# One decoder layer on one core: the mixer and branch stage with all five engines in source order instead of two

## The chip, the core and the metric

The kernel is one program on one core of a Trainium2 chip. A core has five engines, each with its own queue of instructions: TensorE (PE in the profile, PEld for its weight loads), VectorE (DVE), ScalarE (ACT), GpSimd (POOL) and SyncE (SP), which here only issues DMAs. An engine takes its queue from the front; an instruction that has to wait for a semaphore holds everything behind it on that engine. The metric is device time in microseconds (us) of one execution; three runs of the kernel before gave 1828.75, 1835.99 and 1836.97, a median of 1835.99.

## The reference

One layer of a decoder trunk is applied to a prompt of 256 tokens and to 8 single tokens ("samples") that continue stored states; the width is 2048, everything is float32. In outline:

```
h = rmsnorm(x) * (1 + sc1) + sh1                  # sc, sh, gt come from silu(c) @ w_ada
z = h @ w_in                                      # one wide projection for three mixers and their gates
A: u, v = gelu(z_uv);  v = layernorm(v);  y_a = u * (causal 128x128 mix of v per group + b)
B: HGRN2 gated linear recurrence, 8 heads of 128  (chunked, decay = exp of cumulative log gates)
C: GLA gated linear recurrence, 4 heads, value width 256
merged = sum over n of sigmoid(z_gate[n]) * (branch[n] @ w_branch[n])
x = x + gt1 * rmsnorm(merged @ w_out)
x = x + gt2 * rmsnorm(square(relu(h2 @ w_mlp_up)) @ w_mlp_down),  h2 as h, with sc2 and sh2
```

Outputs are the new rows of prompt and samples, the final states of both recurrences for prompt and samples, and the normalised v rows of the samples.

## The kernel before

**The large products.** The 264 tokens (256 + 8) are the moving side of every large product, weights are the stationary side. A float32 weight is split in two float32r parts, hi and lo, and a product is three matmuls: hi by hi (L659), hi by lo (L660), lo by hi (L661). The unit of work is the *granule* (function `granule`, L649): 4 row blocks of 128 by 256 columns of a weight, 512 KB, 24 matmuls. All weights of the kernel form one list (`plan`), and `Stream` walks it: SP loads an item of the list into a `raw` buffer (L616), then `split_half` makes the two halves of the item: ACT copies raw to `whi` (L109), DVE subtracts to get `wlo` (L106, both in `split`). There are four `raw` buffers and six half buffers each of `whi` and `wlo`, that is three items. `Stream.ahead` is called before and after the matmuls of each granule. After granule p it writes the split of item p+3 and the load of item p+6 into the source. The halves of item p+3 take the buffers of the halves of item p, so that the first ACT copy can start when PE is in the middle of granule p and the second when it is at its end.

**The work beside them.** The three mixers are Python generators: `mixer_a` (L881), and `mixer_r` (L1121) for two HGRN2 groups of four heads and for GLA. Their small matmuls, transposes and elementwise steps are put between granules. `linear` (L716) calls `background()` after every granule, which is one *tick*: the counter `now` goes up by one, the queue `bg` (mixers) and the queue `bs` (sample states, `samples_r`) are pumped by their current rates, and `slot()` places collected small matmuls (the level matmuls L679, the samples' matmuls L686) and the modulation matmuls of w_ada (L376), whose weights `Rounds.load` fetches (L339, on SP). A bare `yield` in a generator costs one unit of the rate; `yield READY` waits for the next tick; `yield lambda` waits for a condition. In this way the order of the source already has a distance of ticks between a step and its user: the matrices of a level are used two ticks later or more, the sample state of a step three ticks after its load was issued (`FETCHED`), a value row two.

**Places that the prediction uses.** In `mixer_a`: after `to_tokens` of v, a one-column matmul (L896) ends in a copy (L897); then for each of two token halves two `bn_stats` (L902), `bn_aggr` (L904), eleven one-column steps of a reciprocal root (L213 to L219), the normalisation (L908) and two products with rows (L100, L103 by `mul` and `add`); then the same layer norm for the samples, which starts with three copies (L919, L920) and three folds, whose result PE sums over partitions (L244). In `mixer_r`: the copies of the masked level results into `att` (L1183), the blocks of 32 and 64 (L1192, L1195, then PE at L1208), the scaling of the head outputs (a reciprocal root, then L1285) before their transposes (L1294). In `samples_r`: GpSimd fetches a state `st` (L1077) and a value row `vbc` (L1083), ACT scales the state (L1103), DVE adds the outer product (L1105), GpSimd stores it (L1106). Each branch ends with a gate: `branch` (L1334) has tanh on ACT (L1340) and the gated product on DVE (L1347, L1349). `parts_b` and `parts_c` (L1371 and L1378) finish branches B and C: for C two samples' transposes (L1307) with copies (L1308), then for each of two blocks four products (L1385) and one split of the whole block into hi and lo (an ACT copy and a DVE subtraction of 1056 columns). PE then runs four granules of a gate projection before it needs that block.

**What sets the order.** The source is traced once, and a scheduler orders each engine's queue: it takes instructions in source order as its own forecast of times says that they are ready. Inside `tc.manual_schedule(engines=...)` the engines named keep the order of the source. The kernel uses it in stages, and each stage names other engines. The stage at hand starts at L969, where the generators of the mixers are started, and ends at L1404, behind the last branch. Inside it run GLA's projections (`gla_group`), the three branches and both gate projections: 210 granules. PE and GpSimd keep the order of the source there; DVE, ACT and SP have the scheduler's.

Of the kernel before, what the change touches and what calls it, by code (L numbers as in the profile page):

```python
# [57 lines left out]
def hybrid_step_kernel(  # L58
# [67 lines left out]
    order = tc.manual_schedule(engines={mybir.EngineType.PE, mybir.EngineType.SP, mybir.EngineType.Pool})  # L126
# [659 lines left out]
    every = [mybir.EngineType.PE, mybir.EngineType.SP, mybir.EngineType.Pool, mybir.EngineType.DVE, mybir.EngineType.Activation]  # L786
    order = tc.manual_schedule(engines=set(every))
# [19 lines left out]
    order = tc.manual_schedule(engines=set(every[0:3]))  # L807
# [73 lines left out]
    def mixer_a():  # L881
# [71 lines left out]
        for gp in range(4):  # L953
# [12 lines left out]
            )  # L966
            V.scalar_tensor_tensor(u[:, :, 0:NP], yv[:, :, 0:NP], 0.5, u[:, :, 0:NP], ALU.mult, ALU.mult)
            yield
    order = tc.manual_schedule(engines={mybir.EngineType.PE, mybir.EngineType.Pool})  # L969
    order.__enter__()  # L970
    gen_a = mixer_a()
    bg.g.append(gen_a)
# [499 lines left out]
    order = tc.manual_schedule(engines={mybir.EngineType.PE})  # L1472
# [25 lines left out]
    order = tc.manual_schedule(engines={mybir.EngineType.PE, mybir.EngineType.DVE, mybir.EngineType.Activation})  # L1498
# [161 lines left out]
    order = tc.manual_schedule(engines={mybir.EngineType.PE})  # L1660
# [100 lines left out]
```

## Time and profile before

| | before |
|---|---|
| median of three runs | 1835.99 us |
| profiled execution, its own time | 1832.18 us |
| its span | 1830.4 us |
| PE busy in the span | 1788.7 us (98%) |
| DVE busy | 1181.8 us (65%) |
| ACT busy | 1000.3 us (55%) |
| POOL busy | 131.3 us (7%) |
| the stage at hand, first to last large matmul | 293.3 to 1000.4 us |

PE times are pipelined: a matmul is drawn 277 ns long, and in the steady part of the trace one starts every 0.112 us, so that a granule takes 2.7 us. An engine's idle time in brackets, as in [0.73 <-PE mm L660], is what it waited ahead of that instruction, and for whom. PEclk in a window is the clock granted to PE as a share of full speed.

### The profile page before, as it was taken

To read this page: it belongs to the slowest core of one execution; us is meant where nothing else is said; L and a number is where in the kernel's file an instruction comes from. 1 tells how busy PE (TensorE), PEld (TensorE's weight loads), DVE (VectorE), ACT (ScalarE), POOL (GpSimd) and SP (SyncE) were. 2 spreads that over 40 slices of the span, in tenths; PEclk is the share of its full clock that TensorE was granted. 3 is DMA by queue.
4 is the path that set the end of the run, shared out by engine and by line. 5 is a ranking of instruction groups with operands and counts; after the bars stand their busy time and mean duration, and the time that the engine had idled before them with its cause. 6 is when DMAs were issued, how large, how long until landed. Compare 5 with 4: busy or idle time off the path is not lost.

```text
span 1830.4 us, 42186 instructions
## 1 busy us (share of the span) xinstructions
PE 1788.7 (98%) x17012; PEld 1696.5 (93%) x17012; DVE 1181.8 (65%) x2092; ACT 1000.3 (55%) x1818; POOL 131.3 (7%) x210
## 2 busy tenths in 40 slices
PE   6999999999999999999999999999999999999998
PEld 4889999989988999989999989999999999999997
DVE  4566677787576696566555667555666666666666
ACT  5544364666755765654445666555554545454544
POOL 4221000111111101210000000000000000000000
PEclk9999999999999999999999999999999999999999
DMA  9999697788787788897987964777666666666663
GB/s 326 354 343 304 195 304 231 215 266 276 239 287 233 229 270 278 274 323 250 308 254 265 327 180 146 246 256 227 191 197 194 197 194 196 195 195 196 196 196 106
DMA packets 330179, 442.05 MB, mean 242 GB/s; under 512 B 14946, under 2 KB 276944, under 8 KB 329984
## 3 DMA queue, kind: packets, MB, share of 16 engines
q1 hardware_dynamic: 311728, 380.26, 65.0%
q0 software_dynamic: 17184, 57.85, 9.1%
q8 instruction: 133, 2.18, 0.5%
q10 hardware_dynamic: 1072, 1.25, 0.2%
q14 instruction: 62, 0.51, 0.1%
HBM read 427.60 MB, written 11.70 MB: 240 GB/s over the span
## 4 chain that ended last, share of the span: by engine, by line
PE 88%; DMA 2%; DVE 2%; issue 1%; ACT 1%; POOL 0%; DVEq 0%; ACTq 0%; POOLq 0%
PE mm L659 27%; PE mm L661 26%; PE mm L660 26%; PE ada L376 3%; DMA vbc<-vs_d 1%; PE ada L308 1%; DVE wlo L106 1%; PE sm L851 1%; PE sm L1208 1%; PE sm L679 1%; PE sm L686 1%; DMA raw<-in_w_in_dram 0%; DVE b L106 0%; PE sm L1578 0%; ACT whi L109 0%
## 5 line engine op out<-in xcount | busy, mean ns | idle before, releaser
L659 PE MATMUL mm<-b,whi 128*128 128x264 f32 x4624 | 1292.4, 279 | 12.3 <-issue 5.1
L661 PE MATMUL mm<-b,wlo 128*128 128x264 f32 x4624 | 1279.7, 277 | 5.1 <-DVE wlo L106 4.5
L660 PE MATMUL mm<-b,whi 128*128 128x264 f32 x4624 | 1278.8, 277 | 0.8 <-DVE b L106 0.7
L106 DVE TENSOR_TENSOR wlo<-raw,whi 128x512 fp32r<-128x512 f32 x1136 | 774.4, 689 | 489.1 <-ACT whi L109 475.0
L109 ACT CAST whi<-raw 128x512 fp32r<-128x512 f32 x1136 | 691.8, 616 | 644.5 <-DVE wlo L106 331.7
L659 PEld LDWEIGHTS mm<-b,whi 128*128 128x128 f32 x4624 | 875.8, 189 | 53.0 <-issue 28.0
L661 PEld LDWEIGHTS mm<-b,wlo 128*128 128x128 f32 x4624 | 876.2, 189 | 7.3 <-DVE wlo L106 7.2
L660 PEld LDWEIGHTS mm<-b,whi 128*128 128x128 f32 x4624 | 876.2, 189 | 4.4 <-issue 3.0
L103 DVE TENSOR_TENSOR b<-b,mm 128x528 f32<-128x528 f32 (+1 forms) x137 | 95.7, 699 | 24.5 <-PE mm L661 13.0
L1105 DVE SCALAR_TENSOR_TENSOR st<-vbc,b,st 128x128 f32<-128x128 f32 (+1 forms) x96 | 34.2, 390 | 55.2 <-DMA vbc<-vs_d 50.4
L1103 ACT ACTIVATE st<-st,fs 128x128 f32<-128x128 f32 (+1 forms) x96 | 37.1, 430 | 50.5 <-DMA st<-in_state_hgrn_dram 26.9
L488 POOL DMA_DIRECT2D b<-in_w_ada_dram x64 | 46.2, 724 | 126.0 <-PE ada L308 94.4
L376 PE MATMUL ada<-araw,cT 128*32 128x512 f32 x296 | 39.8, 601 | 0.0
L308 PE MATMUL ada<-b,cT 128*32 128x256 f32 (+1 forms) x640 | 35.1, 356 | 2.8 <-DMA b<-in_w_ada_dram 2.6
L100 DVE TENSOR_TENSOR b<-b,b 128x512 f32<-128x512 f32 (+1 forms) x47 | 33.9, 741 | 1.3 <-ACT b L1221 1.0
L1106 POOL DMA_DIRECT2D out_dram<-st x32 | 23.6, 736 | 130.5 <-DVE st L1105 130.5
L308 PEld LDWEIGHTS ada<-b,cT 128*32 128x32 f32 x640 | 17.8, 113 | 14.9 <-DMA b<-in_w_ada_dram 6.2
L376 PE MATMUL ada<-b,cT 128*32 128x512 f32 x216 | 26.2, 594 | 0.0
L106 DVE TENSOR_TENSOR b<-gt,b 128x528 fp32r<-128x528 f32 x32 | 22.7, 710 | 3.2
L106 DVE TENSOR_TENSOR b<-b 128x1024 f32<-128x1024 f32 (+1 forms) x24 | 24.3, 1017 | 0.0
L1632 ACT ACTIVATE b<-vt 128x528 fp32r<-128x528 f32 x32 | 23.0, 719 | 1.0
L106 DVE TENSOR_TENSOR b<-b,b 128x1056 fp32r<-128x1056 f32 (+3 forms) x21 | 20.8, 991 | 4.0 <-ACT b L109 3.8
(344 smaller groups left out, 854.0 us busy)
## 6 DMA issues: line engine op xcount, KB each, us to landing
raw<-in_w_in_dram SPq DMA_DIRECT2D x231, 512.0 KB, 4.8
raw<-in_w_mlp_up_dram SPq DMA_DIRECT2D x128, 512.0 KB, 3.9
raw<-in_w_mlp_down_dram SPq DMA_DIRECT2D x128, 512.0 KB, 3.7
araw<-in_w_ada_dram SPq DMA_DIRECT2D x74, 512.0 KB, 5.7
b<-in_w_ada_dram SPq DMA_DIRECT2D x54, 512.0 KB, 6.6
b<-in_w_ada_dram POOLq DMA_DIRECT2D x48, 512.0 KB, 8.9
raw<-in_w_branch_dram SPq DMA_DIRECT2D x48, 512.0 KB, 4.5
raw<-in_w_out_dram SPq DMA_DIRECT2D x32, 512.0 KB, 5.3
```

The source lines that it names most:

```text
L100: V.tensor_tensor(o, a, b, op=ALU.mult)
L103: V.tensor_tensor(o, a, b, op=ALU.add)
L106: V.tensor_tensor(o, a, b, op=ALU.subtract)
L109: S.copy(hi, src)
L308: T.matmul(acc[32 * j:32 * j + 32, 0:n], cT[:, k, :], w[:, n * j:n * j + n], start=k == 0, stop=k == KT - 1)
L376: T.matmul(self.acc[32 * j:32 * j + 32, :], cT[:, k, :], ws[j // 2][:, j % 2 * 512:j % 2 * 512 + 512], start=k == 0, stop=k == KT - 1)
L488: queue.dma_start(w[:, i], w1[k * P:(k + 1) * P, :, self.k0 * P:(self.k0 + self.n) * P])
L659: T.matmul(o, a, xh(k + j), start=first and j == 0, stop=False)
L660: T.matmul(o, a, xl(k + j), start=False, stop=False)
L661: T.matmul(o, b, xh(k + j), start=False, stop=last and j == n - 1)
L1103: S.activation(st[:, i, :], st[:, i, :], AF.Copy, scale=fs[:, h0 + i, b:b + 1])
L1105: V.scalar_tensor_tensor(st[:, i, :], v[:, i, :], k[:, h0 + i, NP + b:NP + b + 1], st[:, i, :], ALU.mult, ALU.add)
```

## The change

From L969 to the end of the branches the queues of all five engines keep the order of the source. `every` is the list [PE, SP, Pool, DVE, Activation] that an earlier stage already defined. No instruction is added or removed.

```
-    order = tc.manual_schedule(engines={mybir.EngineType.PE, mybir.EngineType.Pool})
+    order = tc.manual_schedule(engines=set(every))
     order.__enter__()
     gen_a = mixer_a()
     bg.g.append(gen_a)
```

More of the change, by code (lines that the diff above doesn't have):

```diff
@@ L968, in mixer_a @@
             yield
-    order = tc.manual_schedule(engines={mybir.EngineType.PE, mybir.EngineType.Pool})
+    order = tc.manual_schedule(engines=set(every))
     order.__enter__()
```

## The prediction

> **What bounds the kernel now.** The page comes first, then the windows of the stage at hand (293.3 to 1000.4 us) and of a steady later stage.
>
> ```profile
> span 1830.4 us, 42186 instructions
> ...
> L106 DVE TENSOR_TENSOR wlo<-raw,whi 128x512 fp32r<-128x512 f32 x1136 | 774.4, 689 | 489.1 <-ACT whi L109 475.0
> L109 ACT CAST whi<-raw 128x512 fp32r<-128x512 f32 x1136 | 691.8, 616 | 644.5 <-DVE wlo L106 331.7
> ```
>
> ```profile
> 293.30:1000.40 707.10, 696.52 (x7156) 648.81 (x7156) 480.58 (x895) 419.93 (x812) 73.05 (x111) 1.00 0.81 263
> 1300.00:1700.00 400.00, 400.00 (x3558) 400.00 (x3558) 250.08 (x370) 201.84 (x330) 0.00 (x0) 1.00 0.65 196
> ```
>
> PE bounds. In the stage it works 696.5 of 707.1 us, so at most 10.6 us of idle can be won there, while nothing limits what can be lost. The steady window gives the pitch: 400 us over 3558 matmuls is 0.112 us, and a granule of 24 takes 2.7 us. A split costs ACT 2 x 0.62 and DVE 2 x 0.69 us per granule; DVE is busy 480.6 us (68%). Next, PE's waits from 360 to 1060 us, and the waits of DVE and ACT for sample states:
>
> ```profile
> PE mm L659 <- issue: 5.1, 2, 2.9
> PE mm L661 <- DVE wlo L106: 4.3, 5, 2.3
> PE mm L659 <- ACT whi L109: 0.3, 1, 0.3
> ```
>
> ```profile
> DVE st L1105 <- DMA vbc<-vs_d: 50.4, 19, 7.4
> ACT st L1103 <- DMA st<-in_state_hgrn_dram: 26.9, 7, 7.2
> ACT st L1103 <- DMA st<-in_state_gla_dram: 16.9, 9, 3.5
> ```
>
> The scheduler put L1103 and L1105 ahead of where the source has them, before their DMAs land: 94.2 us of waiting at the head of DVE's and ACT's queues, with splits behind. One such place, around 675 us, and below it PE's two other gaps over 2 us:
>
> ```profile
> 673.03 0.69 DVE L106 TENSOR_TENSOR wlo<-raw,whi 128x512 fp32r<-128x512 f32 x1
> 678.16 0.88 DVE L1105 SCALAR_TENSOR_TENSOR st<-vbc,b,st 128x256 f32<-128x256 f32 x2 [4.44 <-DMA vbc<-vs_d]
> 675.67 0.91 ACT L1103 ACTIVATE st<-st,fs 128x256 f32<-128x256 f32 x2 [3.14 <-DMA st<-in_state_gla_dram]
> 677.49 1.12 ACT L109 CAST whi<-raw 128x512 fp32r<-128x512 f32 x2
> 678.16 0.38 PE L659 MATMUL mm<-b,whi 128*128 128x264 f32 x1 [2.19 <-issue]
> 565.89 0.27 PE L659 MATMUL mm<-b,whi 128*128 128x264 f32 x1 [2.86 <-issue]
> 807.34 0.38 PE L661 MATMUL mm<-b,wlo 128*128 128x264 f32 x1 [2.26 <-DVE wlo L106]
> ```
>
> PE's gap ahead of 678.16 is called "issue", but it ends when the first cast of 677.49 does: it belongs to the state wait. The "issue" gap ahead of 565.89 comes with no such wait; I leave it where it is.
>
> **The change part by part.** *Nothing is added or removed*, so the sums are waits alone. PE and POOL keep their order.
>
> *Gain: the state waits go.* In source order L1103 and L1105 stand three and two ticks behind the issue of their DMAs and behind the splits of their tick. PE's share of the waits is 4.3 + 0.3 + 2.2 = 6.8 us. The clock adds to it:
>
> ```profile
> 566.00:571.00 5.00, 5.00 (x31) 5.00 (x31) 3.12 (x7) 3.90 (x10) 0.30 (x1) 0.66 0.56 193
> 679.00:684.00 5.00, 5.00 (x78) 4.95 (x65) 5.00 (x11) 2.75 (x6) 0.00 (x0) 0.66 0.68 207
> 808.00:813.00 5.00, 5.00 (x48) 4.46 (x47) 5.00 (x9) 1.24 (x2) 0.00 (x0) 1.00 0.92 270
> ```
>
> After two of the three gaps over 2 us PE had 0.66 of its clock for 5 us, which costs 0.34 x 5 = 1.7 us; after the third (ahead of 807.34) it had all of it. The gap at 676 is one of the two, so the gain is 6.8 + 1.7 = 8.5 us.
>
> The Trainium skill, "TensorE: Matmul & The Clock Gate", section "HAM oscillation — how this bites in real kernels", has the rule "no PE-idle gaps >~3.4µs". By it gaps of 2.2 and 2.9 us would cost no clock; the windows above disagree, and the sum goes by them. It is weighed as a rival below.
>
> *Loss: mixer work falls behind the splits.* A split of tick p waits for PE: its second cast starts when granule p ends. In source order everything of tick p stands behind it, so DVE starts that work 0.62 + 0.69 = 1.3 us after granule p ended; before, the scheduler let it overtake. That is harmless where the user comes two ticks (5.4 us) later. I went through PE's small matmuls in source order and found these places late.
>
> *Layer norm of mixer A.*
>
> ```profile
> 306.87 0.62 ACT L109 CAST whi<-raw 128x512 fp32r<-128x512 f32 x1 [0.73 <-PE mm L660]
> L896 PE MATMUL sm<-b,cst x2: 251/262/272, 306.9 to 307.0; 1*128 1x8 f32 x2
> 298.40 0.68 DVE L902 BATCH_NORM_STATS2 bst<-b 128x6 f32<-128x512 f32 x1
> 313.22 0.20 DVE L904 BATCH_NORM_AGGREGATE bag<-bst 128x2 f32<-128x12 f32 x1
> 316.59 0.81 DVE L908 TENSOR_SCALAR b<-b,bag,lnr 128x1024 f32<-128x1024 f32 x1
> 317.92 1.22 DVE L100 TENSOR_TENSOR b<-b,b 128x1024 f32<-128x1024 f32 x1
> 320.79 1.89 DVE L106 TENSOR_TENSOR wlo<-raw,whi 128x512 fp32r<-128x512 f32 x3
> L919 DVE COPY vsa<-b x2: 182/182/182, 253.6 to 259.0; 128x32 f32<-128x32 f32 x2
> L244 PE MATMUL sm<-vsb,cst x4: 173/214/256, 322.0 to 324.9; 128*128 128x8 f32 x4
> ```
>
> In the source L902 follows the matmul L896 (306.9), and the samples' copies L919 follow the norm of both token halves; here L902 began at 298.4, and L919 ran at 253.6. In source order DVE starts L902 after the cast of 306.87 and its subtraction, at 308.1. Until PE's L244 it then has two halves of: two L902 at 0.6, L904 to L908 2.15 (313.22 to 316.59, less two subtractions of 0.61), L908 0.75, L100 and L103 1.14 each (starts 0.08 closer than their length): 6.4 each, 12.8. Further eight subtractions at 0.61, 4.9, and six samples' steps at 0.2, 1.2. It is done at 308.1 + 18.9 = 327.0; PE reaches L244 at 322.0. **Loss 5.0.**
>
> *Branch C's end.*
>
> ```profile
> L1307 PE MATMUL sm<-cst,os x4: 272/273/273, 639.5 to 859.0; 128*128 128x128 f32 x4
> L1385 DVE SCALAR_TENSOR_TENSOR b<-b,vec,b x8: 486/487/494, 859.4 to 863.5; 128x264 f32<-128x264 f32 x8
> L106 DVE TENSOR_TENSOR b<-b,b 128x1056 fp32r<-128x1056 f32 x9 | 11.3, 1253 | 1.9 <-ACT b L109 1.9
> L109 ACT CAST b<-b 128x1056 fp32r<-128x1056 f32 x9 | 10.9, 1211 | 1.0 <-DVE b L1375 0.7
> L1364 DVE SCALAR_TENSOR_TENSOR b<-b,mm x8: 690/697/705, 601.9 to 860.4; 128x528 f32<-128x528 f32 x8
> ```
>
> The tick's granule ends at 859.0. Then, in order: cast 0.6, tanh 0.6, L1364 0.6, two copies 0.4 (861.2), four L1385 1.6, the ACT copy 1.2, the subtraction 1.2, four L1385 1.6, the second copy 1.2 (868.0), its subtraction 1.2 (869.2) and only now the next split's first half, 0.7: 869.9. PE wants it three granules after 859.0, at 867.2, its third matmul at 867.4. **Loss 2.5.** Branch B's end has the same form with only one copy exposed, and scans behind it; I take 1.6.
>
> *Blocks of 32, and head scaling.*
>
> ```profile
> 434.26 1.89 PE L1208 MATMUL sm<-b 128*128 128x64 f32 x16
> 431.17 1.65 ACT L1183 COPY att<-a 32x256 f32<-32x256 f32 x4 [1.98 <-DVE a L1154]
> 426.18 0.99 ACT L1103 ACTIVATE st<-st,fs 128x128 f32<-128x128 f32 x3
> L1294 PE MATMUL sm<-cst,b x32: 272/273/273, 483.7 to 772.6; 128*128 128x128 f32 x32
> L1285 ACT ACTIVATE b<-b,rr 128x128 f32<-128x128 f32 x16 | 5.3, 391 | 1.5 <-DVE rr L219 1.5
> ```
>
> L1208 comes two granules after its chain's tick ended (434.3 - 5.4 = 428.9). The chain: cast 0.6, L1183 1.65, exp, subtraction, exp 0.6 each, four L1103 at 0.33, last L1105 0.35, gate 0.6, two subtractions 1.2, product 0.7: 8.2, so 437.1. Loss 2.8; in the third group 2 (no L1183 just ahead, a fuller DVE); in the second, other PE work ahead of it covers the chain. L1294: from 478.3 (483.7 - 5.4) split 1.3, root 2.15, four L1285 1.3, two casts 1.2, four L1285 1.3: 485.5, loss 1.8, and 1.2 in the second group.
>
> *State DMAs in their new place.* They land in 5.8 to 6.5 us (median) and at worst 9, against some 8 us of distance; the trace does not show it. Bounds: 0, and the 6.8 that they cost now. I take 2, nearer the median.
>
> *SP.* Weight loads (L616) stand before w_ada's loads (L339) of a tick. An L339 waits for PE's L376 of its own tick, and the L616 behind it for a split one tick younger, so nothing is lost: 0, and, if `raw` ran dry, one landing (4.7 us) at a time. The order of Ln and Exp on ACT is the same in both, so no table load is added: 0.
>
> Sum of losses: 5.0 + 2.5 + 1.6 + 2.8 + 2 + 1.8 + 1.2 + 2 = 18.9. Three of the gaps exceed 2.3 us; at 1.7 each the clock adds 5.1. Net 24.0 - 8.5 = +15.5 us. The profiled execution took 1832.2 (span 1830.4, 1.8 around it), 3.8 under the median of 1836.0; it becomes **1848**, 0.65% over that median.
>
> **The rivals.**
> *Faster.* The state waits were all there was, and mixer chains are hidden as the ticks intend: 1832.2 - 8.5 = 1824. It decides at L244: if DVE ends the samples' folds before 322, it holds. For it: 94.2 us of waits. Against it: PE feels 6.8 of them, and the 18.9 us of DVE work ahead of L244 fit in no 13.9.
> *No change.* Half the losses, one clock loss: 1832.2 + 9.5 + 1.7 - 8.5 = 1835. For it: PE ran through DVE waits of 7.4 us, so its lead of three granules is worth something.
> *Much slower.* States still land late, and now no split can pass: gain 0, losses half as much again (28), six clock losses (10): 1870. Against it: the two and three ticks.
> *The clock costs less.* Gaps between 2 and 3.4 us cost no clock, and only L244's does: +18.9 + 1.7 - 6.8 = 1846. This is the rule of the Trainium skill's clock gate page. Two rows of 0.66 speak against it.
> That the change does nothing is excluded: L902 and L919 stand elsewhere than in the source.
>
> **How the numbers follow.** Forecast 0.45 (own range 1840 to 1858), much slower 0.13, clock 0.04, no change 0.29, faster 0.09. A measurement tells about 0.5% (9 us) from no change: faster below 1826.8, slower above 1845.2. Slower 0.45 + 0.13 + 0.02 = 0.60, same 0.29 + 0.02 = 0.31, faster 0.09. The low end takes half the losses and the unexplained gap gone with its clock loss (1835 - 4.6 = 1830), the high end is the much slower case.
>
> **What would show it.** Right: DVE and ACT wait under 20 us for vbc and st; L902 starts after 308; PE waits for DVE ahead of L244 for about 5 us, ahead of L1208 and L1294 for 2 to 3, and for a split about 8 us after L1307. Wrong: L244 without a wait, the vbc waits still there, or PE waiting for SP's loads or for PSUM's readers, which I cost at nothing.

## The result, and the profile after

The changed kernel takes 1859.37 us (median of 4 runs, 1857.04 to 1861.91) against 1836.48 for the kernel before beside it: ratio 1.0136, 95% interval 1.0117 to 1.0154. It is 22.9 us slower, where the prediction's 1848 lay 12 us above the median of before. The profiled execution took 1858.75 us.

The page of the changed kernel, with the two halves of a split:

```profile
span 1857.0 us, 42257 instructions
...
L106 DVE TENSOR_TENSOR wlo<-raw,whi 128x512 fp32r<-128x512 f32 x1136 | 769.7, 689 | 542.7 <-ACT whi L109 530.9
L109 ACT CAST whi<-raw 128x512 fp32r<-128x512 f32 x1136 | 688.7, 617 | 674.3 <-DVE wlo L106 341.1
```

The splits cost what they did; only idle time has grown. The same stage as a window (length, then the busy time of PE, PEld, DVE, ACT and POOL, PEclk, DMA share, GB/s):

```profile
294.50:1026.90 732.40, 706.73 (x7156) 656.74 (x7156) 488.00 (x901) 418.38 (x812) 72.79 (x111) 0.98 0.80 254
```

The stage went from 707.1 to 732.4 us: 25.3 of the 26.6 us between the two profiled executions. With the same 7156 matmuls, PE's idle time went from 10.6 to 25.7 us (+15.1), and its busy time from 696.5 to 706.7 (+10.2): matmuls are drawn longer, above all under half the clock. PE's waits in the stage (total, times, longest):

```profile
PE sm L244 <- DVE vsb L103: 5.7, 1, 5.7
PE sm L686 <- DVE st L1105: 5.2, 2, 4.0
PE mm L659 <- ACT whi L109: 3.7, 2, 2.4
PE sm L1208 <- DVE b L100: 3.4, 3, 1.9
PE sm L1294 <- ACT b L1285: 3.3, 3, 1.9
PE mm L661 <- DVE wlo L106: 2.5, 3, 0.9
PE mm L660 <- issue: 1.8, 1, 1.8
```

All the named places are there, and one that was not named, L686. (The `issue` line is the gap that stood ahead of 565.89 before; it is now 1.8 us.) Of the waits of DVE for vbc and of ACT for st, 94.2 us before, 0.4 us are left. In their place the heads of the two queues now wait for other steps:

```profile
DVE st L1105 <- ACT st L1103: 7.5, 7, 1.7
DVE b L106 <- PE sm L679: 5.7, 1, 5.7
DVE st L1105 <- DMA vbc<-vs_d: 0.4, 1, 0.4
```

```profile
ACT b L1168 <- DVE b L106: 32.9, 12, 6.8
```

*L244.* DVE's timeline ahead of it, and PE's:

```profile
327.87 0.26 DVE L919 COPY vsa<-b 128x32 f32<-128x32 f32 x2
328.17 0.20 DVE L920 COPY vsb<-vsa 128x64 f32<-128x64 f32 x1
328.39 0.60 DVE L103 TENSOR_TENSOR vsb<-vsb 128x32 f32<-128x32 f32 x3
```

```profile
329.05 0.59 PE L244 MATMUL sm<-vsb,cst 128*128 128x8 f32 x2 [5.71 <-DVE vsb L103]
```

The samples' copies stand behind the norms of both token halves, as in the source; they end at 329.0, two microseconds later than the 327.0 of the prediction. PE came later too: it stood ready at 323.3 (329.05 less 5.71) in place of 322.0, since the stage itself began 1.2 us later.

*L686, which was not predicted.* The timeline of DVE, ACT and PE:

```profile
558.65 1.23 DVE L106 TENSOR_TENSOR b<-b 128x1024 f32<-128x1024 f32 x1 [5.73 <-PE sm L679]
559.79 0.70 DVE L1347 SCALAR_TENSOR_TENSOR b<-gt,mm 128x528 f32<-128x528 f32 x1
559.91 0.63 ACT L1168 ACTIVATE b<-b 128x512 f32<-128x512 f32 x1 [6.79 <-DVE b L106]
...
562.81 1.13 DVE L1105 SCALAR_TENSOR_TENSOR st<-vbc,b,st 128x128 f32<-128x128 f32 x4
563.21 0.97 PEld L686 LDWEIGHTS sm<-st,b 128*32 128x32 f32 x8 [4.16 <-DVE st L1105]
563.21 1.42 PE L686 MATMUL sm<-st,b 128*32 128x128 f32 x8 [4.04 <-DVE st L1105]
```

A mixer step (a subtraction through L106 that feeds L1168) stood at the head of DVE for 5.7 us until PE had done L679. In the source it reads nothing that PE makes; it writes a fresh block (L1162) of the pool of 28, and the L679 read such blocks of earlier levels. So it waited for a block that those L679 still read. This is concluded from the source and the wait; the trace names no buffer. Behind it stood the rest of the tick, and L1105 last; PE needed that L1105 for the L686 of the same slot, right behind L679. The source leaves a distance of ticks there, but a step that waits for a block has none. A larger pool was not tried.

### The profile page after: what moved, and what is told of

Its sections match the earlier page's. It is cut to its first block, busy times and chain, and to the rows that moved or that the text cites. A ratio compares the mean times of both kernels' runs of the same rounds, so it can differ in the third digit from the quotient of the medians.

```text
span 1857.0 us, 42257 instructions
## 1 busy us (share of the span) xinstructions
PE 1797.5 (97%) x17012; PEld 1704.0 (92%) x17012; DVE 1187.9 (64%) x2092; ACT 998.5 (54%) x1818; POOL 131.0 (7%) x210
## 4 chain that ended last, share of the span: by engine, by line
PE 86%; DVE 3%; ACT 3%; issue 1%; DMA 1%; DVEq 0%; ACTq 0%
PE mm L659 26%; PE mm L660 26%; PE mm L661 26%; PE ada L376 3%; DVE wlo L106 1%; ACT whi L109 1%; PE ada L308 1%; PE sm L1208 1%; PE sm L851 1%; DMA raw<-in_w_branch_dram 1%; PE sm L686 1%; PE sm L679 0%; ACT b L109 0%; PE sm L1578 0%; DVE b L106 0%
## 5 line engine op out<-in xcount | busy, mean ns | idle before, releaser
L106 DVE TENSOR_TENSOR wlo<-raw,whi 128x512 fp32r<-128x512 f32 x1136 | 769.7, 689 | 542.7 <-ACT whi L109 530.9
L1106 POOL DMA_DIRECT2D out_dram<-st x32 | 23.5, 736 | 262.2 <-DVE st L1105 258.8
L1105 DVE SCALAR_TENSOR_TENSOR st<-vbc,b,st 128x128 f32<-128x128 f32 (+1 forms) x96 | 32.7, 391 | 8.1 <-ACT st L1103 7.5
L1103 ACT ACTIVATE st<-st,fs 128x128 f32<-128x128 f32 (+1 forms) x96 | 34.8, 426 | 0.0
L106 DVE TENSOR_TENSOR b<-b 128x1024 f32<-128x1024 f32 (+1 forms) x24 | 24.4, 1018 | 5.8 <-PE sm L679 5.7
L106 DVE TENSOR_TENSOR b<-b,b 128x1056 fp32r<-128x1056 f32 (+3 forms) x21 | 20.8, 992 | 8.5 <-ACT b L109 8.2
L109 ACT CAST b<-b 128x1056 fp32r<-128x1056 f32 (+2 forms) x18 | 17.0, 950 | 16.4 <-DVE b L103 7.1
L1168 ACT ACTIVATE b<-b 128x512 f32<-128x512 f32 x12 | 7.7, 646 | 32.9 <-DVE b L106 32.9
```

The lines of the kernel that those rows point to most:

```text
L106: V.tensor_tensor(o, a, b, op=ALU.subtract)
L109: S.copy(hi, src)
L1103: S.activation(st[:, i, :], st[:, i, :], AF.Copy, scale=fs[:, h0 + i, b:b + 1])
L1105: V.scalar_tensor_tensor(st[:, i, :], v[:, i, :], k[:, h0 + i, NP + b:NP + b + 1], st[:, i, :], ALU.mult, ALU.add)
```

## The experiments

The theory is that of the prediction: the change gains the state steps' waits and loses wherever the source leaves a chain too short a distance, at each place for its own reason. The rivals are that one engine's queue (SP's loads among them) carries the loss, and that the gain comes from the order as a whole and not from the state steps.

**One engine more at a time.** Three kernels, which differ from the kernel before in the engines named:

```
-    order = tc.manual_schedule(engines={mybir.EngineType.PE, mybir.EngineType.Pool})
+    order = tc.manual_schedule(engines={mybir.EngineType.PE, mybir.EngineType.Pool, mybir.EngineType.DVE})
     # the second: Activation in place of DVE; the third: SP in place of DVE
```

> PE, GpSimd and DVE keep the source order, ACT and SP have the scheduler's. My theory (the loss is DVE's: mixer steps stand behind the splits, and one wait at the head of DVE's queue holds everything): DVE's wait for vbc is gone, PE waits about 5.7 us ahead of L244 as in the changed kernel, and the time is 1848 to 1860. Rival (the loss needs DVE and ACT together, since each waits for the other): 1836 to 1843, within 0.4% of before.

> PE, GpSimd and ACT keep the source order, DVE and SP have the scheduler's. My theory: no wait of PE ahead of L244, since DVE may take the samples' steps early; the wait ahead of L1294 stays (it is ACT's); ACT's 43.8 us of waits for st are gone and with them part of the gain: 1828 to 1840. Rival (ACT's order carries the loss, by its casts that stand ahead of everything): 1848 or more.

> PE, GpSimd and SP keep the source order, DVE and ACT have the scheduler's. My theory: SP's order costs and gives nothing, 1832 to 1840, PE's gaps as before. Rival (w_ada's loads stand in the way of weight loads): DVE and ACT wait for raw, over 1845.

The vector engine alone: 1882.15 us, ratio 1.0264 (1.0249 to 1.0280), slower than all five engines together; both expectations missed. The scalar engine alone: 1838.42, ratio 1.0024 (1.0015 to 1.0034). In that kernel DVE, whose order is the scheduler's, also stands 4.9 us for L679 and PE 3.7 us at L686, so this loss does not need DVE in source order. The sync engine alone: 1834.98, ratio 1.0007 (0.9998 to 1.0016). So SP's order costs nothing, as the prediction had it. The timeline of the first kernel at its longest wait of PE shows how it loses time:

```profile
448.93 0.40 ACT L1103 ACTIVATE st<-st,fs 128x128 f32<-128x128 f32 x1 [3.84 <-DMA st<-in_state_hgrn_dram]
449.23 0.60 ACT L109 CAST whi<-raw 128x512 fp32r<-128x512 f32 x1
449.74 0.98 ACT L1103 ACTIVATE st<-st,fs 128x128 f32<-128x128 f32 x3
449.87 0.69 DVE L106 TENSOR_TENSOR wlo<-raw,whi 128x512 fp32r<-128x512 f32 x1 [6.45 <-ACT whi L109]
...
456.68 1.11 PE L1208 MATMUL sm<-b 128*128 128x64 f32 x4 [7.96 <-DVE b L100]
```

ACT, still free, has L1103 early and waits 3.8 us for its state; the cast behind it comes late; DVE may take nothing else meanwhile and stands for 6.5 us at that cast's subtraction; then PE waits 8.0 us at L1208.

**A longer way to L244.** Two more ticks before the samples' sum over partitions, in the changed kernel:

```
+        yield READY
+        yield READY
         ps = sum_partitions(w8, NS)          # mixer_a; holds L244
```

> The changed kernel with two more ticks between the samples' folds and PE's sum over partitions in mixer A (two more yields READY ahead of the first L244). My theory (PE arrives there 5.7 us before DVE, and pays that and some 2 us of clock): the wait ahead of L244 falls below 0.5 us, the clock dip at 326 us goes, and the time falls by 6 to 8 us to 1851 to 1853. Rival (DVE simply has too much to do there, and the next user waits instead): the time stays within 2 us of 1859, with new waits between 325 and 350 us.

Measured 1844.58 us, ratio 1.0059 (1.0044 to 1.0074): 14.8 us under the changed kernel, more than expected (the kernel before beside it was 2.3 us faster than beside the changed kernel, so the two figures do not compare to the last microsecond). By the starts of the granules in the two traces the place itself gave 7.8 us (granules 8 and 9): L244 waits 0.56 us in place of 5.7, and the half clock behind it is gone. The rest goes with the mixers running two ticks later, and no run takes it apart: the first L1208, for one, waits 0.7 in place of 1.9 us. A new wait appears, 2.3 us for a tanh on ACT. The cause of L244's wait is shown; the 14.8 us are not its price alone.

**Other distances.** In the changed kernel, samples wait one tick longer before the slot reads them:

```
-        sv = [x for x in samples if x[0] + AGE <= now[0]]
+        sv = [x for x in samples if x[0] + AGE + 1 <= now[0]]
```

> The changed kernel with the samples' matmuls (L686) one tick older: a state is taken by a slot three ticks after it was updated instead of two, so that they no longer share the slot with the level matmuls that DVE waits for. Theory (at granule 72 a subtraction at the head of DVE's queue waits for the block of a level tile that PE's L679 of that very slot still reads; L1105 stands behind it and L686 waits for L1105): DVE's wait of 5.7 us for L679 stays, PE's waits ahead of L686 (4.0 and 1.1 us) fall below 0.5, the clock dip at 562 us goes, the time falls by 5 to 8 us to 1851 to 1854. Rival (L1105 is late because DVE has too much to do): PE's wait moves with it and stays over 2 us.

1852.3 us, ratio 1.009 (1.006 to 1.012). The waits of L686 for L1105 are gone from the trace. DVE still stands 5.72 us at its step for PE's L679, so at L686 this wait did its harm through the L1105 behind it. New waits take back a part: 1.6 us for wlo and 1.0 for a tanh, and L1208 waits 3.6 in place of 1.9 us.

In the changed kernel, the ends of branches B and C: GLA's gates start two ticks later, and branch C does all its eight products before its two splits:

```
+        if G.i == 2:
+            yield READY
+            yield READY
         yield from G.gates()
...
                 V.scalar_tensor_tensor(o[:, hd, :], o[:, hd, :], glanT[:, j:j + 1], g, ALU.mult, ALU.mult)
+        for o in Gs[2].o:
             a, b = blk(dt=F32R), blk(dt=F32R)
```

> The changed kernel with two edits far from one another. One: GLA's gates start two ticks later, so that their Ln and its table load no longer stand on ACT between the last gate projection and its tanh at the end of branch B. Theory: the wait at granule 101 (2.4 + 0.9 us) falls below 1. Two: in the end of branch C all eight products are issued ahead of the two splits, so that one ACT copy runs beside four products. Theory: the wait at granule 165 (1.3 + 0.9) falls by 1.2 to about 1. Together 3 to 5 us, 1854 to 1857. Rival for both (the queue is just long): the waits stay within 0.5 us of what they were.

1851.57 us, ratio 1.0086 (1.0059 to 1.0113): 7.8 us under the changed kernel. Both waits of PE for a split, 3.3 us near 671 and 2.2 near 891, are gone. For the first one ACT's timeline of the changed kernel has the cause:

```profile
661.86 1.28 ACT L980 ACT_TABLE_LOAD   x1
663.16 1.08 ACT L980 ACTIVATE b<-b 128x1056 f32<-128x1056 f32 x1
664.26 1.28 ACT L1363 ACT_TABLE_LOAD   x1
665.55 0.61 ACT L1363 ACTIVATE b<-mm 128x528 f32<-128x528 f32 x1
```

GLA's logarithm (L980) stands ahead of the tanh that ends branch B, and each of the two needs its own table. The kernel loads no more tables than before, but in this order two loads and the logarithm, 3.6 us, lie in the chain from L1307 to PE's next split. One load of 1.3 us lay there before too (at 640.18), so that the order adds 2.4 us.

**All distances at once.** The three edits together, and one more tick before L1294:

> All five engines in source order with the ticks of the source moved: two more ticks ahead of L244, one more ahead of L1294, L686 one tick older, GLA's gates two ticks later, the products of branch C ahead of its splits. Nothing else is changed. Theory (the loss is a handful of distances that are too short, and what is left is the gain of the state waits): PE's gaps in the stage sum to under 9 us, at most two clock dips, 1826 to 1834, as fast as before or up to 0.5% faster. Rival (source order on DVE and ACT costs by itself): over 1838.

1841.89 us, ratio 1.0034 (1.0021 to 1.0048): the rival's number. Each named wait is gone or smaller, and PE's gaps are still 17 us, now in front of other users (5.7 us of waits for a tanh, 3.8 at L679, 2.3 at L851). The short distances are not three or four flaws in the source; there are more of them than were repaired.

**The gain without the loss.** The kernel before, all engines as there; only the state steps are tied behind the last split that the source issues ahead of them:

```
     def split(src, hi, lo):
-        S.copy(hi, src)
-        sub(lo, src, hi.bitcast(F32))
+        cut[:] = [S.copy(hi, src), sub(lo, src, hi.bitcast(F32))]     # sub returns its instruction
+    def behind(i, c): tc.add_manual_dep(i.ins, c.ins.name, ORDER, reason="behind the last split")   # order only, no wait
...
-                S.activation(st[:, i, :], st[:, i, :], AF.Copy, scale=fs[:, h0 + i, b:b + 1])
+                behind(S.activation(st[:, i, :], st[:, i, :], AF.Copy, scale=fs[:, h0 + i, b:b + 1]), cut[0])
...          # L1105 likewise: behind(V.scalar_tensor_tensor(...), cut[1])
```

> The kernel before, with only the state steps held: each of the scales on the scalar engine (L1103) and updates on the vector engine (L1105) may not stand ahead of the last split that the source issues before it; every other instruction of the two engines stays free to be moved. Theory (the gain of the change is the state steps' waits for their transfers, its loss is everything else that lost its freedom): the waits of the vector engine for vbc and of the scalar engine for st, 50.4 and 43.8 us before, fall under 15 us; the gains seen in the changed kernel in granules 31 to 145 (14 us together) come without its losses (39 us), so 1822 to 1830 us. Rival (the 14 us come from the whole order, not from the state steps): 1832 to 1838 us. Second rival (held state steps come late for the slots that read them, as in granule 72 of the changed kernel): waits of L686 for L1105, over 1838 us.

**1818.53 us, ratio 0.9910 (0.9896 to 0.9925): it beats both kernels**, by more than was expected. Its stage as a window, and all of PE's waits in it:

```profile
293.60:986.90 693.30, 690.21 (x7156) 644.90 (x7156) 483.87 (x895) 424.02 (x812) 73.14 (x111) 1.00 0.83 268
```

```profile
PE mm L659 <- issue: 1.5, 1, 1.5
PE sm L679 <- issue: 1.4, 1, 1.4
```

PE idles 3.1 us in place of 10.6, and the 7156 matmuls take 690.2 us in place of 696.5: 13.8 us, with no stretch of half clock left in the stage. By the granules' starts the 13.8 us arise at granules 31, 66 to 68, 78, 109, 139 and 145, the places where the changed kernel too is faster than before.

**The sync engine left out of the change.**

> The change without the sync engine: tensor engine, GpSimd, vector and scalar engine keep the order of the source, the sync engine's queue of loads does not. Theory (the sync engine's order costs and brings nothing): 1855 to 1862 us, as the changed kernel, with the 5.7 us wait of L244 and the 4 us wait of L686 at their places. Rival (the loads' order costs part of the 23 us): under 1852 us. With the vector engine alone at 1882 us and the scalar engine alone at 1838 us, both rules also say that the two do not add up: what the vector engine's queue loses alone, it loses to the scalar engine's early state scales.

1857.41 us, ratio 1.0132 (1.0112 to 1.0152), with the waits of L244 and L686 in place. SP takes no part in the loss.

**Which of the two state steps.** Holding L1103 alone should give the same queues as holding both, since L1105 needs its result; it was not run. Holding L1105 alone:

> The kernel before with only the updates on the vector engine (L1105) held behind the last split; the scales on the scalar engine (L1103) may stand early again. (Holding L1103 alone gives the same five queues as holding both, since L1105 needs its result.) Theory (the scalar engine's early scales hold the casts behind them, and these waits are what the tensor engine felt): the scalar engine still waits for st at about 44 us, the vector engine's 50 us for vbc are gone, and at most half of the 17 us gain is there: 1826 to 1838 us. Rival (the vector engine's waits for vbc did the harm): 1816 to 1823 us, as with both held.

1841.89 us, ratio 1.0048 (1.0030 to 1.0066): the theory's side, and beyond its range; none of the gain is there, and the kernel is a little slower than before. Timeline of POOL, ACT and PE at its worst place:

```profile
784.76 0.71 POOL L1106 DMA_DIRECT2D out_dram<-st  x1 [8.87 <-DVE st L1105]
785.47 0.73 POOL L1077 DMA_DIRECT2D st<-in_state_gla_dram  x1
```

```profile
792.11 0.51 ACT L1103 ACTIVATE st<-st,fs 128x256 f32<-128x256 f32 x1 [7.68 <-DMA st<-in_state_gla_dram]
```

```profile
794.30 1.03 PE L686 MATMUL sm<-st,b 128*32 128x256 f32 x2 [4.03 <-DVE st L1105]
```

The later L1105 holds the store L1106 at the head of POOL's queue, the next state's load stands behind it, and ACT, whose L1103 still stands early, waits 7.7 us for that load with the casts behind it. Holding L1105 alone therefore brings a harm of its own, and the run does not tell how much of the 17 us each of the two waits was worth.

**The vector engine fixed, the scalar engine's state scales held.** The queue of DVE is that of the 1882 us kernel:

> Tensor engine, GpSimd and vector engine in source order, and on the scalar engine only the state scales L1103 held behind the last cast; the vector engine's queue is that of the run with the vector engine alone, which gave 1882 us. Theory (that run lost its further 23 us over the changed kernel to the scalar engine's early state scales, which then held the vector engine's fixed queue): the waits of the scalar engine for st go under 10 us, L1208's 8 us wait and all waits of L686 but those of the changed kernel go, L244's 5.7 us stays: 1848 to 1862 us. Rival (the fixed vector queue loses as much to other scalar work that the scheduler moves): over 1870 us.

1841.98 us, ratio 1.0042 (1.0027 to 1.0057), 40 us under that kernel and lower than expected. ACT's waits for st are gone. L244's 5.7 us and one L686's 4.0 us are still there:

```profile
PE sm L244 <- DVE vsb L103: 5.7, 1, 5.7
PE sm L686 <- DVE st L1105: 4.0, 1, 4.0
PE mm L661 <- DVE wlo L106: 3.4, 2, 2.4
PE sm L871 <- DVE srow L868: 2.2, 2, 1.5
```

With this run the change comes apart. State steps late everywhere, medians in us; the kernel before, measured beside them, had medians of 1834.2 to 1835.6:

| | ACT free | ACT in source order |
|---|---|---|
| DVE free | 1818.5 | 1838.4 |
| DVE in source order | 1842.0 | 1857.4 |

Source order for DVE costs 19 to 23.5 us and for ACT 15 to 20. Starting from 1818.5 the two alone cost 23.5 and 19.9, together 43.4, and both at once 38.9: they nearly add up. Holding the state steps gains 17 (1835.6 to 1818.5).

## Why the prediction was right and wrong

The sign, the place and the mechanism were right: state waits go, mixer steps fall behind the splits, and the loss is the larger. The net of 15.5 us came out as 25.3 in the stage, since losses of 24.0 were 39.1: with the state steps held and all else free the stage takes 693.3 us, and the changed kernel's takes 732.4. These losses are 22.6 us of PE's idle time (25.7 less 3.1) and 16.5 of its busy time (706.7 less 690.2). The step that failed most is the clock's term, "Three of the gaps exceed 2.3 us; at 1.7 each the clock adds 5.1". In its place stand 16.5 us of longer busy time, of which 11.7 us are half clock. It accounts for most of the miss: it lacked 11.4 us and the idle time 3.7 (22.6 for 18.9), and the gain was 5.3 larger than forecast.

- **"Gain 8.5".** Measured 13.8. The idle part was right (7.5 for 6.8); the clock and slower matmuls gave 6.3 in place of 1.7. The kernel before had two stretches of half clock of 3.4 us each in the stage, 3.4 us of cost, and the term counted one of them. The gap ahead of 565.89, which I left where it is, was part of it: it fell to 1.5 us in the kernel with held states, and the half clock behind it went.
- **Layer norm of mixer A, "Loss 5.0".** 5.7 us at L244, on the chain that was written down.
- **Blocks of 32 and head scaling.** L1208: 1.9 and 1.1 us for 2.8 and 2. L1294: 2.6 (two waits) and 0.6 for 1.8 and 1.2. Sum 6.2 against 7.8.
- **Branch C's end, "Loss 2.5".** 2.2 us.
- **Branch B's end, "I take 1.6".** 3.3 us. That term was taken from C's without its own chain, and "no table load is added: 0" looked at the count of table loads, not at where they stand.
- **"State DMAs in their new place", "I take 2".** As DMAs they cost nothing: the two and three ticks suffice. But the L1105 cost 5.2 us at L686, for other reasons. Of these, 4.0 us came from a step ahead of it that waited for a block; I had looked at distances in ticks and not at the number of blocks. The other 1.1 us, ahead of 426.77, came from a L1103 that stood behind a mixer step (L1174), which had itself waited 4.3 us for DVE.
- **"At 1.7 each the clock adds 5.1".** Three gaps over 2.3 us were counted. The stage has five stretches of half clock, behind gaps from 1.1 us up, and three of them last 6.8 us, not 3.4. They cost 2.3 us each on average, 11.7 together.
- **SP at nothing.** Right, by two runs.

Windows of the changed kernel: the first five lie on its stretches of half clock, which follow gaps of 5.7, 1.9, 4.0, 1.1 and 1.3 + 0.9 us; the last lies behind the gaps of 2.4 + 0.9 us near 672. PEclk is the share before the last two numbers:

```profile
326.37:333.20 6.83, 4.15 (x19) 4.15 (x20) 5.03 (x18) 0.62 (x1) 0.00 (x0) 0.50 0.67 200
445.84:452.67 6.83, 6.83 (x34) 6.83 (x33) 2.62 (x5) 1.97 (x4) 0.00 (x0) 0.50 0.64 199
561.89:568.72 6.83, 5.51 (x27) 4.88 (x28) 6.80 (x18) 4.20 (x11) 3.06 (x5) 0.50 0.73 211
729.15:732.56 3.41, 3.41 (x18) 3.41 (x18) 1.94 (x4) 1.97 (x4) 0.00 (x0) 0.50 0.75 232
892.99:896.40 3.41, 3.41 (x18) 3.41 (x17) 2.68 (x5) 0.98 (x3) 0.00 (x0) 0.50 0.68 190
673.50:678.50 5.00, 5.00 (x47) 5.00 (x46) 4.97 (x9) 0.62 (x2) 0.00 (x0) 1.00 0.78 257
```

In the five PE is busy for 4.15 + 6.83 + 5.51 + 3.41 + 3.41 = 23.3 us, and at 0.50 of its clock half of that is lost: 11.7 us of the 16.5. Most of the other 4.8 us lies at the gaps themselves, also at full clock:

```profile
671.58 0.38 PE L659 MATMUL mm<-b,whi 128*128 128x264 f32 x1 [2.44 <-ACT whi L109]
671.80 0.28 PE L660 MATMUL mm<-b,whi 128*128 128x264 f32 x1
```

The second matmul behind this gap starts 0.22 us after the first, not 0.11. The matmul ahead of a gap is drawn 0.277 us long, 0.165 more than the 0.112 after which the next would have started. That is about 0.27 us for each gap. PE's waits number 15 in the changed kernel and 2 in the one with held states, so 13 gaps more make 3.5 us, an estimate. About 1.3 us stay open.

Of the rivals, "the clock costs less" fell, since its rule let these gaps go free. The faster rival was right that the state waits alone bring a gain (13.8 us in the stage for its 8.5) and wrong that nothing else would be late. The much slower rival named what happened in the kernel with the vector engine alone: states still late, and no split can pass.

## What to carry to other kernels

Before a queue is put in source order, follow for each user on the bounding engine everything that then stands ahead of its last input, and also what each of those steps waits for, free buffers and table loads included; distances counted in ticks show neither. When a scheduler puts steps ahead of their DMA, tie down those steps, from the first user of the DMA on: here tying both state steps gained 17 us, tying only the second of them lost 7, and tying down everything lost 23. Reckon with half clock behind each new gap on the TensorE, also when the gap is only 1 or 2 us: here it followed at five of nine places with a gap over 1 us and cost 2.3 us each.

## What the hardware showed that was not expected

A gap's length does not tell whether half clock follows. In the changed kernel's stage a gap of 1.14 us and the gaps of 1.27 and 0.88 us near 891 were followed by it, and the 2.44 and 0.88 us near 672 were not; the gap of 1.9 us at L1208 was followed by 6.83 us of it. The stretches of half clock last 3.41 or 6.83 us, and they start 119.47, 116.05, 167.26 and 163.84 us apart: 35, 34, 49 and 48 times 3.413. So they lie on one grid, and where in it a gap falls may matter. What decides stays open: PE idled for 1.14 us of the step ahead of the stretch at 729.15, and for 1.97 us of the step from 667.71, which had none behind it. The Trainium skill, "TensorE: Matmul & The Clock Gate", section "What's actually happening", describes an activity window that runs freely, of about 3.4 us; the lengths of the stretches and the grid of their starts agree with that. That gaps shorter than such a window were enough does not agree with the rule of 3.4 us which the prediction weighed.

The effect of two fixed queues is not the sum of the effects of one: against the kernel before, DVE's order cost 48 us, ACT's 4 and both 22. Only with the early state scales out of the way (the table) do the costs nearly add.
